# A batched matrix product: the deliberately uneven DMA load moved from the first store into the first x, and the last transposes moved forward

## Chip, cores, metric

One core of a Trainium2 chip. The metric is the device time of the program in microseconds (us), the lower the better. All runs told here are in the fast state. Ratios are the mean time of one kernel's fast runs over that of the other's of the same rounds, with a 95% interval, so they are not quite the ratio of the medians that are quoted beside them. The rounds ran on several chips; each ratio is to the kernel before on the same chip. A transfer is split over the 16 DMA engines; the part of one engine is called its share here, and a trace records when each share has landed.

## The reference

```python
def setup_inputs():
    batch, m, k, n = 32, 512, 1024, 768
    return {"x": randn(batch, m, k) as float32, "weight": randn(batch, k, n) as float32}

def reference(x, weight):
    return np.matmul(x, weight).astype(np.float32)
```

32 independent products of 512x1024 by 1024x768. The inputs are 168 MB and the output is 50 MB, so the time goes mainly into moving data.

## The kernel before

x and the weights are loaded on the GpSimd queue, which casts them to bf16, two batches of x and one batch of weights at a time. TensorE transposes x, multiplies, and the results go out as float32. Two details matter. The very first x is loaded as float32 by SyncE in one transfer. And a part of the first output is stored in 25 small transfers that use only a few DMA engines ("SKEWED").

```python
    w_pool = tile_pool(name="w", bufs=4);  x_pool = tile_pool(name="x", bufs=3)
    ...
    def transpose_first(mt):
        xT = xT_pool.tile([P, JT, P, 2], BF16, name="xT")
        for h in range(2):
            pt = tpsum.tile([P, JT, P], F32, name="pt")
            for i in range(JT):
                nc.tensor.transpose(pt[:, i, :], x_first[:, mt, JT * h + i::KT], ident)
            nc.vector.tensor_copy(...)          # cast to bf16
        return xT
    ...
    def store(b):
        cols = MT * N
        if b == SKEWED:
            cols -= 512
            for first in range(0, 120, 20):
                for at in range(first, first + 4):
                    rows = slice(at, first + 20, 4)             # 5 rows: 5 DMA engines
                    nc.sync.dma_start(out_view[b, rows, cols:], outs[b][rows, cols:])
            nc.sync.dma_start(out_view[b, 120:, cols:], outs[b][120:, cols:])
        nc.gpsimd.dma_start(out=out_view[b, :, :cols], in_=outs[b][:, :cols])

        x_first = x_pool.tile([P, MT, K], F32, name="x_sb")
        nc.sync.dma_start(x_first, x_view[0])
        load_w(0); load_pair(1); load_w(1); load_w(2); load_pair(3)
        for b in range(B):
            # GpSimd issues, in this order: the x pair ahead, load_w(b + 3), the store of b - 1
            ...
            if b == 0:
                xT = {mt: transpose_first(mt) for mt in range(MT)}
            elif b == B - 1:
                xT = {mt: transpose_last(mt) for mt in range(MT)}
            ...
```

A weight buffer is free for `load_w(b + 3)` only when TensorE is done with batch b - 1, and the x pair of batches 5 and 6 goes into the buffer of `x_first`. So the issue of loads follows TensorE.

Of the kernel before, what the change touches and what calls it, by code (L numbers as in the profile page):

```python
# [13 lines left out]
def kernel(  # L14
# [6 lines left out]
    nc = tc.nc  # L21
    B, M, K = x.shape
    _, _, N = weight.shape
    P = 128
    MT = M // P
    KT = K // P
# [3 lines left out]
    AHEAD = 3  # L30
    LATE = 4
    HELD = 3
    SKEWED = 0

    const = ctx.enter_context(tc.tile_pool(name="const", bufs=1))
    w_pool = ctx.enter_context(tc.tile_pool(name="w", bufs=4))
# [10 lines left out]
    x_view = x.rearrange("b (mi mo) k -> b mi mo k", mi=P)  # L47
    pair_view = x[1:B - 1].rearrange("(p r) (mi mo) k -> p (r mi) mo k", r=2, mo=2 * MT)
    out_view = out.rearrange("b (mi mo) n -> b mi (mo n)", mi=P)

    xs, ws, outs = {}, {}, {}

    def banks():
        return [mpsum.tile([P, 512], F32, name=f"pm{i}") for i in range(3)]

    def load_pair(b):

        xs[b] = x_pool.tile([P, 2 * MT, K], BF16, name="x_sb")
        nc.gpsimd.dma_start(out=xs[b], in_=pair_view[b // 2])  # L59

    def load_last():
        xs[B - 1] = x_pool.tile([P, MT, K], BF16, name="x_sb")
        nc.gpsimd.dma_start(out=xs[B - 1], in_=x_view[B - 1])  # L63

    def load_w(b):
        ws[b] = w_pool.tile([P, KT, N], BF16, name="w_sb")
        at = 0
        for n in CHUNKED.get(b, (KT,)):
            nc.gpsimd.dma_start(out=ws[b][:, at:at + n, :], in_=w_view[b, :, at:at + n, :])  # L69
            at += n  # L70


    def words(b, mo):
        pt = tpsum.tile([P, JT, P], F32, name="pt")
        pairs = xs[b].bitcast(F32)
        for j in range(JT):
            nc.tensor.transpose(pt[:, j, :], pairs[:, mo, j::JT], ident)  # L77
        return pt.bitcast(BF16)

    def transpose_pair(b, mt):  # L80

        both = xT_pool.tile([P, 2, JT, P // 2, 2, 2], BF16, name="xT")
        for half in range(2):
            nc.vector.tensor_copy(  # L84
                both[:, :, :, :, half, :].rearrange("p b j i r -> p j b i r"),
                words(b, mt + MT * half).rearrange("p j (b i r) -> p j b i r", b=2, r=2),
            )
        return [both[:, r].rearrange("p j i h r -> p j (i h) r") for r in range(2)]

    def transpose_last(mt):  # L90
        xT = xT_pool.tile([P, JT, P, 2], BF16, name="xT")
        nc.vector.tensor_copy(  # L92
            xT.rearrange("p j m r -> p (j m r)"), words(B - 1, mt).rearrange("p j m -> p (j m)")
# [10 lines that stand above are left out]
            nc.vector.tensor_copy(  # L104
                xT[:, 2 * h:2 * h + 2].rearrange("p j m r -> p j r m"),
                pt.rearrange("p (j r) m -> p j r m", r=2),
            )
        return xT
# [8 lines left out]
    def matmuls(pm, half, xT, b, kos, together):  # L117
        for ko in kos:
            for i, (bank, at, off, size) in enumerate(SPLITS[half]):
                shares = half == 1 and i == 0  # L120
                nc.tensor.matmul(  # L121
                    pm[bank][:, at:at + size],
                    xT[:, ko // 2, :, ko % 2],
                    ws[b][:, ko, off:off + size],
                    start=(ko == 0 and not (together and shares)),
                    stop=(ko == KT - 1),
                    skip_group_check=together,
                )

    def evacuate(b, pair, pm):  # L130
        o = outs[b][:, pair * N2:(pair + 1) * N2]
        nc.scalar.copy(o[:, 0:512], pm[0])  # L132
        nc.vector.tensor_copy(o[:, 512:1024], pm[1])  # L133
        nc.scalar.copy(o[:, 1024:N2], pm[2])  # L134

    def store(b):
        cols = MT * N
        if b == SKEWED:

            cols -= 512  # L140
            for first in range(0, 120, 20):
                for at in range(first, first + 4):
                    rows = slice(at, first + 20, 4)
                    nc.sync.dma_start(out_view[b, rows, cols:], outs[b][rows, cols:])
            nc.sync.dma_start(out_view[b, 120:, cols:], outs[b][120:, cols:])
        nc.gpsimd.dma_start(out=out_view[b, :, :cols], in_=outs[b][:, :cols])  # L146

    with tc.manual_schedule():
        x_first = x_pool.tile([P, MT, K], F32, name="x_sb")
        nc.sync.dma_start(x_first, x_view[0])  # L150
        load_w(0)
        ident = const.tile([P, P], F32)
        make_identity(nc, ident)
        load_pair(1)
        load_w(1)
        load_w(2)
        load_pair(3)

        ready = {}
        pending = []  # L160
        for b in range(B):
            if b % 2 and b + AHEAD + 1 < B:
                if b + AHEAD + 1 == B - 1:
                    load_last()
                else:
                    load_pair(b + AHEAD + 1)
            if b + AHEAD < B:
                load_w(b + AHEAD)
            if b <= B - LATE:
                if b > 0:  # L170
                    pending.append(b - 1)
                if b + AHEAD < B - HELD or b == B - LATE:
                    for at in pending:
                        store(at)
                    pending = []
            if b == B - 1:
                halves = [slice(pair * N2, (pair + 1) * N2) for pair in range(2)]
                nc.sync.dma_start(out_view[b - 1, :, halves[0]], outs[b - 1][:, halves[0]])
                for late in range(B - LATE, B - 2):
                    nc.sync.dma_start(out_view[late], outs[late])  # L180
                nc.sync.dma_start(out_view[b - 1, :, halves[1]], outs[b - 1][:, halves[1]])
            outs[b] = out_pool.tile([P, MT * N], F32, name="out_sb")
            if b == 0:
                xT = {mt: transpose_first(mt) for mt in range(MT)}
            elif b == B - 1:
                xT = {mt: transpose_last(mt) for mt in range(MT)}
            else:
                if b % 2:
                    for mt in range(MT):
                        ready[b, mt], ready[b + 1, mt] = transpose_pair(b, mt)  # L190
                xT = {mt: ready.pop((b, mt)) for mt in range(MT)}
            if b not in CHUNKED:
                for pair in range(2):
                    pm = banks()
                    for half in range(2):
                        matmuls(pm, half, xT[2 * pair + half], b, range(KT), False)
                    evacuate(b, pair, pm)
                continue
            pms = [banks() for _ in range(2)]
            at = 0  # L200
            for n in CHUNKED[b]:
                last = at + n == KT
                for mt in range(MT):
                    matmuls(pms[mt // 2], mt % 2, xT[mt], b, range(at, at + n), True)
                    if last and mt % 2 == 1:
                        pair = mt // 2
                        evacuate(b, pair, pms[pair])
                        if b == B - 1:
                            nc.sync.dma_start(out_view[b, :, halves[pair]], outs[b][:, halves[pair]])
                at += n  # L210
# [30 lines left out]
```

## Time and profile before

| | before |
|---|---|
| median of 6 runs (range) | 516.35 us (515.49 to 518.96) |
| HBM traffic | 218.1 MB, 423 GB/s over the span |
| TensorE busy | 85% |
| DMA engines | full from 2 us to about 510 us |
| slowest share of the last store lands | 515.0 us, the fastest 510.6 |

The page, the chain and the last stretches are shown in the prediction. Two more views matter afterwards: what TensorE waited for (total us, times, longest), and when GpSimd issued its transfers (start, duration, the wait ahead of it in brackets). In the views `pt` is the result of transposes, `pm` that of matmuls, `w_sb` weights and `x_sb` x.

```profile
PE pm L121 <- DMA w_sb<-in_weight_dram: 43.3, 12, 5.4
PE pt L103 <- DMA x_sb<-in_x_dram: 12.3, 1, 12.3
```

```profile
19.52 0.53 POOL L59 DMA_DIRECT2D x_sb<-in_x_dram  x1 [14.38 <-PE pt L103]
29.92 0.53 POOL L69 DMA_DIRECT2D w_sb<-in_weight_dram  x1 [9.87 <-PE pm L121]
...
45.98 0.53 POOL L69 DMA_DIRECT2D w_sb<-in_weight_dram  x1 [14.70 <-PE pm L121]
```

The x pair of batches 5 and 6 is issued at 19.5 us, the weights of batch 4 at 29.9 and those of batch 5 at 46.0. The queue ahead of them (six loads, all issued by 5.1 us, the last of which lands at 58 us) keeps the DMA engines supplied beyond these times.

### The profile page before, as it was taken

Reading aid. Unit: us, or ns where it says so; the run is one execution under the profiler, and the core shown is the slowest. Engines: PE = TensorE matmul, PEld = TensorE weight load, DVE = VectorE, ACT = ScalarE, POOL = GpSimd, SP = SyncE. Lnnn points to the kernel's source line nnn. Section 1 sums busy time; section 2 is a strip of 40 time slices with the busy share of each in tenths; the row PEclk is TensorE's granted clock in tenths of the full one; section 3 lists DMA queues with packets and bytes.
Section 4 is the critical chain, followed back from the end, with each engine's and each line's share of the span. In section 5 each row is a group of like instructions: output and inputs, shape, how many; then the busy total and the mean of one; then the engine's idle time right before and its main releaser. Section 6 shows DMA issues by size and latency. Waiting matters only on the chain.

```text
span 515.9 us, 5853 instructions
## 1 busy us (share of the span) xinstructions
PE 440.0 (85%) x2576; PEld 279.6 (54%) x2576; DVE 129.9 (25%) x196; ACT 76.2 (15%) x129; POOL 43.8 (8%) x87
## 2 busy tenths in 40 slices
PE   0999969979799697996979979898797988999992
PEld 0665635646366364663646636464464644656661
DVE  0541412314132041320413204141041410404131
ACT  0012111111111111111111111111111111111211
POOL 3001000010000100001000010000001100011000
PEclk9999998989899798997999979999798997999998
DMA  8999999999999999999999999999999999999996
GB/s 255 217 219 215 221 255 293 211 279 274 272 283 211 283 268 275 279 213 293 260 273 273 224 295 246 280 278 235 299 233 275 279 250 300 214 277 215 289 426 276
DMA packets 12952, 135.63 MB, mean 263 GB/s; under 512 B 1536, under 2 KB 1536, under 8 KB 3328
## 3 DMA queue, kind: packets, MB, share of 16 engines
q0 software_dynamic: 11664, 126.62, 96.2%
q1 hardware_dynamic: 1264, 8.65, 4.2%
q8 instruction: 20, 0.33, 0.2%
q14 instruction: 4, 0.03, 0.0%
HBM read 167.77 MB, written 50.33 MB: 423 GB/s over the span
## 4 chain that ended last, share of the span: by engine, by line
PE 64%; DMA 21%; DVE 7%; another core or an unknown queue 6%; issue 1%; ACT 0%
PE pm L121 56%; DMA w_sb<-in_weight_dram 19%; PE pt L77 6%; DVE xT L84 4%; DMA x_sb<-in_x_dram 2%; DVE out_sb L133 2%; PE pt L103 1%; DVE xT L104 0%; DVE xT L92 0%; ACT out_sb L134 0%
## 5 line engine op out<-in xcount | busy, mean ns | idle before, releaser
L121 PE MATMUL pm<-w_sb,xT 128*128 128x256 bf16 (+1 forms) x2048 | 358.9, 339 | 43.3 <-DMA w_sb<-in_weight_dram 43.3
L121 PEld LDWEIGHTS <-xT 128*128 128x128 bf16 x2048 | 206.8, 101 | 190.8 <-DMA w_sb<-in_weight_dram 47.9
L133 DVE COPY out_sb<-pm 128x512 f32<-128x512 f32 x64 | 44.3, 691 | 351.4 <-PE pm L121 338.4
L77 PE MATMUL pt<-ident,x_sb 128*128 128x128 f32 x496 | 79.8, 302 | 10.5 <-DVE xT L84 10.2
L132 ACT COPY out_sb<-pm 128x512 f32<-128x512 f32 x64 | 37.5, 585 | 305.9 <-PE pm L121 290.7
L77 PEld LDWEIGHTS pt<-ident,x_sb 128*128 128x128 f32 x496 | 69.3, 209 | 21.5 <-DVE xT L84 18.7
L84 DVE COPY xT<-pt 128x1024 bf16<-128x1024 bf16 x120 | 77.4, 687 | 11.0 <-PE pt L77 11.0
L134 ACT COPY out_sb<-pm 128x512 f32<-128x512 f32 x64 | 37.5, 585 | 124.0 <-PE pm L121 123.9
L69 POOL DMA_DIRECT2D w_sb<-in_weight_dram x37 | 19.7, 533 | 298.2 <-PE pm L121 261.4
L146 POOL DMA_DIRECT2D out_dram<-out_sb x28 | 15.0, 536 | 81.7 <-DMA w_sb<-in_weight_dram 41.9
L103 PE MATMUL pt<-ident,x_sb 128*128 128x128 f32 x32 | 6.7, 362 | 12.5 <-DMA x_sb<-in_x_dram 12.3
L103 PEld LDWEIGHTS pt<-ident,x_sb 128*128 128x128 f32 x32 | 5.1, 205 | 13.9 <-issue 12.2
L59 POOL DMA_DIRECT2D x_sb<-in_x_dram x15 | 8.0, 533 | 45.0 <-DMA out_dram<-out_sb 30.6
L104 DVE CAST xT<-pt 128x512 bf16<-128x512 f32 x8 | 5.8, 736 | 14.2 <-PE pt L103 13.8
L92 DVE COPY xT<-pt 128x1024 bf16<-128x1024 bf16 x4 | 2.6, 686 | 0.2 <-PE pt L77 0.2
L132 ACT ACT_TABLE_LOAD x1 | 1.3, 1283 | 0.7 <-PEq L225 0.7
L63 POOL DMA_DIRECT2D x_sb<-in_x_dram x1 | 0.5, 528 | 6.7 <-DMA w_sb<-in_weight_dram 6.7
masks.py:199 POOL TENSOR_SCALAR_AFFINE_SELECT ident<-ident 128x128 f32<-128x128 f32 x1 | 0.3, 287 | 0.1
masks.py:197 POOL MEMSET ident<- 128x128 f32 x1 | 0.2, 223 | 0.0
L225 POOL MEMSET const-float32-0.0<- 128x1 f32 x1 | 0.1, 98 | 0.2 <-issue 0.2
L225 POOL MEMSET const-bfloat16-1.0<- 128x1 bf16 x1 | 0.1, 101 | 0.0
L225 POOL MEMSET const-uint8-127<- 128x1 uint8 x1 | 0.1, 101 | 0.0
(1 smaller groups left out, 0.1 us busy)
## 6 DMA issues: line engine op xcount, KB each, us to landing
w_sb<-in_weight_dram POOLq DMA_DIRECT2D x28, 1536.0 KB, 47.3
out_dram<-out_sb POOLq DMA_DIRECT2D x27, 1536.0 KB, 46.6
x_sb<-in_x_dram POOLq DMA_DIRECT2D x15, 2048.0 KB, 52.4
w_sb<-in_weight_dram POOLq DMA_DIRECT2D x7, 768.0 KB, 38.4
out_dram<-out_sb SPq DMA_DIRECT2D x4, 768.0 KB
out_dram<-out_sb SPq DMA_DIRECT2D x2, 1536.0 KB
x_sb<-in_x_dram SPq DMA_DIRECT2D x1, 2048.0 KB
out_dram<-out_sb POOLq DMA_DIRECT2D x1, 1280.0 KB, 48.7
```

Of the source, the lines that this page charges most:

```text
L59: nc.gpsimd.dma_start(out=xs[b], in_=pair_view[b // 2])
L69: nc.gpsimd.dma_start(out=ws[b][:, at:at + n, :], in_=w_view[b, :, at:at + n, :])
L77: nc.tensor.transpose(pt[:, j, :], pairs[:, mo, j::JT], ident)
L84: nc.vector.tensor_copy(both[:, :, :, :, half, :].rearrange("p b j i r -> p j b i r"), words(b, mt + MT * half).rearrange("p j (b i r) -> ...
L92: nc.vector.tensor_copy(xT.rearrange("p j m r -> p (j m r)"), words(B - 1, mt).rearrange("p j m -> p (j m)"))
L103: nc.tensor.transpose(pt[:, i, :], x_first[:, mt, JT * h + i::KT], ident)
L104: nc.vector.tensor_copy(xT[:, 2 * h:2 * h + 2].rearrange("p j m r -> p j r m"), pt.rearrange("p (j r) m -> p j r m", r=2),)
L121: nc.tensor.matmul(pm[bank][:, at:at + size], xT[:, ko // 2, :, ko % 2], ws[b][:, ko, off:off + size], start=(ko == 0 and not (together an ...
L132: nc.scalar.copy(o[:, 0:512], pm[0])
L133: nc.vector.tensor_copy(o[:, 512:1024], pm[1])
L134: nc.scalar.copy(o[:, 1024:N2], pm[2])
L146: nc.gpsimd.dma_start(out=out_view[b, :, :cols], in_=outs[b][:, :cols])
```

## The change

Intent: have the uneven load in the first x instead of in the first store, start the first transposes after 1.5 MB instead of 2 MB, and hide the last transposes among the matmuls of batch 30.

```diff
-    def store(b):
-        ... 24 stores of 5 rows x 2 KB and one of 8 rows for b == SKEWED, the rest in one store
-
         x_first = x_pool.tile([P, MT, K], F32, name="x_sb")
-        nc.sync.dma_start(x_first, x_view[0])
+        nc.sync.dma_start(x_first[:, :MT - 1], x_view[0, :, :MT - 1])
+        few = [slice(at, first + 20, 4) for first in (0, 20, 40) for at in range(first, first + 4)]
+        for rows in (slice(64, P), slice(60, 64), *few):
+            nc.sync.dma_start(x_first[rows, MT - 1], x_view[0, rows, MT - 1])
...
-                        store(at)
+                        nc.gpsimd.dma_start(out=out_view[at], in_=outs[at])
...
-                xT = {mt: transpose_first(mt) for mt in range(MT)}
+                xT = {mt: transpose_first(mt) for mt in range(MT - 1)}
             elif b == B - 1:
-                xT = {mt: transpose_last(mt) for mt in range(MT)}
+                xT = last_xT
...
-                        matmuls(pm, half, xT[2 * pair + half], b, range(KT), False)
+                        mt = 2 * pair + half
+                        if mt not in xT:
+                            xT[mt] = transpose_first(mt)
+                        matmuls(pm, half, xT[mt], b, range(KT), False)
...
                 for mt in range(MT):
+                    if last and b == B - 2:
+                        last_xT[mt] = transpose_last(mt)
                     matmuls(pms[mt // 2], mt % 2, xT[mt], b, range(at, at + n), True)
```

More of the change, by code (lines that the diff above doesn't have):

```diff
@@ L32 @@
     HELD = 3
-    SKEWED = 0
     const = ctx.enter_context(tc.tile_pool(name="const", bufs=1))
@@ L134, in evacuate @@
         nc.scalar.copy(o[:, 1024:N2], pm[2])
-    def store(b):
-        cols = MT * N
-        if b == SKEWED:
-            cols -= 512
-            for first in range(0, 120, 20):
-                for at in range(first, first + 4):
-                    rows = slice(at, first + 20, 4)
-                    nc.sync.dma_start(out_view[b, rows, cols:], outs[b][rows, cols:])
-            nc.sync.dma_start(out_view[b, 120:, cols:], outs[b][120:, cols:])
-        nc.gpsimd.dma_start(out=out_view[b, :, :cols], in_=outs[b][:, :cols])
     with tc.manual_schedule():
         x_first = x_pool.tile([P, MT, K], F32, name="x_sb")
-        nc.sync.dma_start(x_first, x_view[0])
+        nc.sync.dma_start(x_first[:, :MT - 1], x_view[0, :, :MT - 1])
+        few = [slice(at, first + 20, 4) for first in (0, 20, 40) for at in range(first, first + 4)]
+        for rows in (slice(64, P), slice(60, 64), *few):
+            nc.sync.dma_start(x_first[rows, MT - 1], x_view[0, rows, MT - 1])
         load_w(0)
@@ L157 @@
         load_pair(3)
-        ready = {}
+        ready, last_xT = {}, {}
         pending = []
```

## The prediction

> **What bounds the kernel now.** I read the page first, then the chain that ended last in order of time, then the busy time by stretch at the end, then SyncE's own waits.
>
> ```profile
> span 515.9 us, 5853 instructions
> PE 440.0 (85%) x2576; PEld 279.6 (54%) x2576; DVE 129.9 (25%) x196; ACT 76.2 (15%) x129; POOL 43.8 (8%) x87
> ...
> DMA  8999999999999999999999999999999999999996
> ...
> HBM read 167.77 MB, written 50.33 MB: 423 GB/s over the span
> ```
>
> The DMA row is 9 from the second slice to the last but one: the 16 DMA engines are never short of work. TensorE is busy 85% of the time, so it has slack somewhere. The traffic is 218.1 MB whatever the order: 13.63 MB on each engine if it is spread evenly.
>
> The chain of waits looks different at its end:
>
> ```profile
> 423.55 3.59 another core or an unknown queue
> 427.14 0.05 issue
> 427.19 12.93 PE pm L121 x63
> ...
> 493.05 0.02 issue
> 493.07 0.70 DVE out_sb L133
> 493.78 0.69 DVE xT L92
> 494.46 0.04 issue
> 494.51 1.35 PE pt L77 x8
> 495.86 10.41 PE pm L121 x64
> 506.27 0.02 issue
> 506.29 0.58 ACT out_sb L134
> ```
>
> From 427 us TensorE waits for no data any more; the transposes of the last x (493.05 to 495.86) and the 64 matmuls of batch 31 stand on this chain, and it ends at 506.87. Taken alone it would promise that any microsecond saved there is saved at the end. But the span ends 9.0 us later, so the stretches after it have to be read:
>
> ```profile
> 500.00:507.00 7.00, 6.25 (x39) 3.54 (x37) 1.38 (x2) 2.30 (x4) 0.00 (x0) 1.00 0.96 408
> 507.00:510.00 3.00, 0.00 (x0) 0.00 (x0) 0.00 (x0) 0.00 (x0) 0.00 (x0) 1.00 1.01 420
> 510.00:513.00 3.00, 0.00 (x0) 0.00 (x0) 0.00 (x0) 0.00 (x0) 0.00 (x0) 0.65 0.51 211
> 513.00:515.00 2.00, 0.00 (x0) 0.00 (x0) 0.00 (x0) 0.00 (x0) 0.00 (x0) 0.50 0.08 34
> ```
>
> The last two columns are the DMA share and GB/s. The DMA engines are full until 510, then they run out one after another. The completion updates in the trace (one for each engine's share of a transfer) say who is last. The last store's 16 shares end at 510.6 to 513.1 for fourteen engines, and 514.5 and 515.0 for the other two. The latest shares of the last four stores end at 509.5, 511.3, 513.1 and 515.0: 1.83 us apart, for 48 KB each, 26.9 GB/s. So the slowest DMA engine has a backlog to the very end, although the last two stores were issued only at 505.6 and 506.9. The early engines instead had a gap (505.7, then 508.7, then 510.6). **The bound is the slowest DMA engine's total work**, and TensorE's end has about 4 us to spare: the slowest engine gets to the last two stores only at about 511.3.
>
> **What the Trainium skill says.** "DMA: Bandwidth & Descriptors", section "Measured", gives 425 GB/s for a 16 MB load; the 423 GB/s above agrees, so there is no rate left to win. Its section "Why a DMA increments its semaphore by 16 and not by 1" says that a transfer runs on the largest number of engines, up to 16, that divides the slowest dimension, and on SyncE's path on the lowest-numbered ones. So 5 rows go to engines 0 to 4, 64 rows to all 16, 4 rows to engines 0 to 3, 8 rows to 0 to 7. The trace agrees in count: 128 packets of 2 KB for 24 x 5 + 8 rows, and each small store shows five completions. After them, in the store at 77 to 79.5 us, five shares are late (79.1 to 79.5, the others 76.9 to 78.2), where earlier transfers had all 16 within 1 us. Its section "Queues, rings and completion order" says that an engine takes turns between queues packet by packet. The trace agrees:
>
> ```profile
> 30.27 37.17 SPq L144 DMA_DIRECT2D out_dram<-out_sb  x24
> 68.27 0.33 SPq L145 DMA_DIRECT2D out_dram<-out_sb  x1
> ```
>
> The small stores landed from 36.0 to 78 us, some 2.0 us apart, far more than 2 KB need: each has two packets (data, completion), and each waits for a GpSimd-queue packet of 0.93 us (a weight row) or 1.23 us (an x row).
>
> **The change, part by part.**
>
> *1. The uneven loading is moved, not altered.* Before: 24 stores of 5 rows x 2 KB and one of 8 rows. Engines 0 to 4 carry 25 x 2 = 50 KB instead of 16 KB (+34 KB), engines 5 to 7 2 KB (-14), engines 8 to 15 none (-16). After: the first x's last row tile is 4 KB a row; an even split would be 32 KB. 64 rows give every engine 16 KB; 4 rows give 4 KB to engines 0 to 3; 12 loads of 5 rows give 48 KB to engines 0 to 4. So engines 0 to 3 have 68 KB (+36), engine 4 64 KB (+32), engines 5 to 15 16 KB (-16). Against before: +2 KB, -2 KB, -2 KB, 0. At 26.9 GB/s 2 KB are 0.08 us. Whichever engine is the slowest, its sum changes by less than 0.1 us. A few packets and completions more or fewer (22 ns each): under 0.3 us.
>
> *2. The start of batch 0.* The first load shrinks from 2.0 to 1.5 MB. Before, it landed at 12.1, the transposes ran 12.27 to 19.2, and the matmuls began when they ended, w having landed at 15.8. After, three tiles are in by about 9.5, transposed by about 15 (24 of 32 transposes, 5.2 of 6.95 us), and the matmuls begin at about 15.5 to 16, some 3 us earlier. Then the fourth tile is missing. Queue turns put its arrival late: the 64 rows take five turns of about 1 us after 5.6 us, the 4 rows two, the 12 small loads 12 x 2 turns at about 2.0 us a load = 24 us: about 34 to 40 us. TensorE wants it at about 24. So I expect TensorE to stand still for 10 to 15 us there, batch 0 to end at 38 to 44 instead of 29.64, and the next x pair (issued at 19.5, when x_first is free) and w of batch 4 (29.9) to be issued as much later.
> Does the DMA queue run dry? No: the fourth weight load lands at 58 before, so the next transfer in the queue, the x pair, is wanted only at about 50. w of batch 5, issued at 46, landed at 87 behind transfers that end at 79.5; issued at 60 it is still in time. TensorE, 12 us late, catches up in the waits for w which it has (43.3 us in 12 waits). By about 150 us it is on the old timetable. Cost at the end: 0.
>
> *3. The last x.* x of batch 31 lands at 474.6; its transposes move from after 493.05 to between the matmuls of batch 30 from 488 on. No new wait. 16 transposes cost 16 x 0.121 = 1.9 us of TensorE wherever they stand; the waits for VectorE between them go (2.60 us from the first transpose to the first matmul, so 0.3 to 0.7 us). TensorE ends at about 506.3 instead of 506.87. Batch 30's two halves are evacuated 1 and 2 us later, and SyncE's stores (491.3 on) start about 1 us later, while the slow engine has GpSimd-queue stores in hand until 504.0. Effect at the end: 0, as the slow engine has 4 us of backlog.
>
> *4. The first store* goes from 1280 to 1536 KB in one transfer, the 256 KB taken from the small stores: counted in 1.
>
> Sum: 0 +- 0.4 us in the slowest engine's work. Prediction 516.8, which is the old median of 517.0 with a token 0.2 off.
>
> **Rivals.** (a) *TensorE's chain sets the end.* For it: the chain of waits from 427 us on. Then the 0.3 to 0.7 us of part 3 come off, and the time is 516.4. Against: the 1.83 us steps of the last stores. (b) *The late fourth tile starves the DMA queue* or the delay lives on to 427 us: the weight loads wait for TensorE's buffers (261.4 us of GpSimd's waits). Each microsecond of dry queue is one at the end; 1 to 5 us, 518 to 522. Against: some 46 us from issue to landing, four weight buffers. (c) *Where the uneven load stands matters*: it sits on five engines from 10 us on instead of from 36 on and takes loads instead of stores, and the slowest engine at the end may be one of the five or not. If the drift between engines (0.7 us of spread at 15 us, 5.6 us at 474) depends on who lags, the end moves by up to 2 us either way, 514.8 to 518.8. Nothing in the profile tells, as it doesn't name engines.
>
> **Range and chances.** The three runs before lie between 515.5 and 519.0, a scatter larger than any term above; it and rival (c) make the range, 514.8 to 518.8. 2% would be 10.3 us: as the bytes on the slowest engine are the same, nothing here can give that, and only a queue dry for 10 us could cost it. Faster by over 2%: 0.01; within 2%: 0.98; slower: 0.01.
>
> **What would show the steps right or wrong.** Right: the DMA row stays at 9; the last store's latest shares end 1.83 us apart; TensorE's first matmul on w at about 16, a gap of 10 us or more before the last 8 transposes of x_first, and later waits for w summing to some 10 us less; the last transposes without VectorE waits; the last matmul about 0.5 us earlier with the span unchanged. Wrong: a DMA slice below 9 between 40 and 120 us (rival b), last stores that start in gaps on all engines (rival a), or a spread of the last store's shares well off 4.4 us (rival c).

## The result and the profile after

| | before | after |
|---|---|---|
| median (range), 6 runs each | 516.35 us (515.49 to 518.96) | 520.01 us (518.30 to 521.52) |
| ratio | | 1.0066 (1.0037 to 1.0096) |

The change costs 3.4 us, and the median lies above the predicted range. The page of the changed kernel:

```profile
span 518.3 us, 5792 instructions
...
DMA  8999999999999999999999999999999999999996
...
HBM read 167.77 MB, written 50.33 MB: 421 GB/s over the span
```

The DMA row looks exactly as before. One slice is 13 us long and 9 means 90% or more, so a loss of one microsecond is invisible there. The waits of TensorE and its order in time show at once where to look:

```profile
PE pt L102 <- DMA x_sb<-in_x_dram: 39.9, 1, 39.9
PE pm L120 <- DMA w_sb<-in_weight_dram: 26.6, 7, 5.1
```

```profile
39.86 5.43 PE L102 MATMUL pt<-ident,x_sb 128*128 128x128 f32 x24 [39.86 <-DMA x_sb<-in_x_dram]
45.13 7.96 PE L120 MATMUL pm<-w_sb,xT 128*128 128x512 bf16 x47
52.93 1.05 PE L102 MATMUL pt<-ident,x_sb 128*128 128x128 f32 x8
54.36 2.77 PE L120 MATMUL pm<-w_sb,xT 128*128 128x256 bf16 x16 [0.38 <-DVE xT L103]
```

The first transpose starts at 39.86 us, not at 12.27 as before and not at 9.5 as predicted. The 1.5 MB load had landed at about 10 us. But the 24 transposes of the first three row tiles waited for the last of the 12 small loads too, which landed at 39.6. There is then no gap before the last 8 transposes (52.93): everything waited at the start. Batch 0 ends at 57.1, 27.5 us later than before, and GpSimd's issues follow:

```profile
54.28 0.53 POOL L58 DMA_DIRECT2D x_sb<-in_x_dram  x1 [49.14 <-PE pt L102]
57.43 0.53 POOL L68 DMA_DIRECT2D w_sb<-in_weight_dram  x1 [2.62 <-PE pm L120]
...
73.50 0.53 POOL L68 DMA_DIRECT2D w_sb<-in_weight_dram  x1 [14.71 <-PE pm L120]
```

The fourth weight load, the last transfer in the queue, was finished by the first DMA engine at 56.0 us. The x pair behind it was issued only at 54.28. Busy time in the stretches 54 to 60 and 70 to 76 us, before and then after (the last two columns are DMA share and GB/s):

```profile
54.00:60.00 6.00, 5.52 (x37) 4.38 (x35) 3.61 (x6) 0.58 (x1) 1.06 (x2) 1.00 1.07 228
70.00:76.00 6.00, 2.15 (x13) 1.08 (x11) 0.69 (x1) 0.65 (x2) 0.53 (x1) 1.00 0.98 269
```

```profile
54.00:60.00 6.00, 5.15 (x33) 3.80 (x33) 3.71 (x7) 0.59 (x1) 1.59 (x3) 1.00 0.98 197
70.00:76.00 6.00, 5.95 (x38) 3.66 (x38) 0.69 (x1) 1.45 (x3) 1.60 (x3) 1.00 0.99 174
```

The loss has two parts. At 54 to 60 us engines really have nothing to do for a moment: between 56.0 and 56.5, on average 10.4 packets are under way instead of 16.5, and the first packets of the x pair then take up to 2.05 us instead of 1.23. At 70 to 76 us the share is full, but packets of the weight load take up to 2.6 us instead of 0.93. A "busy" DMA engine may thus be slow, and GB/s has to be read beside the share. (The GB/s before at 70 to 76 is higher also because stores, which count fully, begin there earlier; for weights the row counts the bf16 bytes written, some 212 GB/s at full rate.)

Where the loss arises shows from the landing times. The median of the 16 shares of each transfer was 0.5 us earlier than before at the fourth weight load (56.4 against 56.9; the kernel before had by then also moved eleven small stores), 0.6 later at the x pair (67.2 against 66.6), 1.9 later at the weights of batch 4 (76.2 against 74.3), 2.7 later at the first store (80.1 against 77.4), and still about 2.5 later at 215 us. So some 2.5 us are lost between 56 and 80 us and are not won back; the two profiled executions differ by 2.4 us in all (518.3 against 515.9). A pair of runs told below, `changed_again` against `contig12`, is cleaner, as both have the same transfers on the same chip: 0.0 us at the fourth weight load, then 1.2, 2.8 and 2.9 later, and 2.8 at 155 us. The slowest share, which sets the end, wanders more: in the first pair it was 1.4 us late at 80 us, 0.0 at 300 and 2.2 at the end; in the second 2.5, 3.8 and (at 500 us) 3.9. So not all of the end's delay is traced to 56 to 80 us.

At the end, the slowest share of the last four stores lands at 511.7, 513.5, 515.3 and 517.2: 1.83 us apart, as before.

### The profile page after: what moved, and what is told of

Its sections match the earlier page's. It is cut to its first block, busy times and chain, and to the rows that moved or that the text cites. A ratio compares the mean times of both kernels' runs of the same rounds, so it can differ in the third digit from the quotient of the medians.

```text
span 518.3 us, 5792 instructions
## 1 busy us (share of the span) xinstructions
PE 427.7 (83%) x2528; PEld 277.2 (53%) x2576; DVE 129.8 (25%) x196; ACT 76.3 (15%) x129; POOL 43.8 (8%) x87
## 4 chain that ended last, share of the span: by engine, by line
PE 61%; DMA 25%; DVE 6%; another core or an unknown queue 3%; issue 1%; SPq 1%; ACT 0%
PE pm L120 54%; DMA w_sb<-in_weight_dram 19%; DMA x_sb<-in_x_dram 7%; PE pt L76 6%; DVE xT L83 4%; DVE out_sb L132 2%; PE pt L102 1%; SPq L141 1%; DVE xT L103 0%; ACT out_sb L133 0%; SPq L138 0%
## 5 line engine op out<-in xcount | busy, mean ns | idle before, releaser
L120 PE MATMUL pm<-w_sb,xT 128*128 128x256 bf16 (+1 forms) x2000 | 347.9, 333 | 29.5 <-DMA w_sb<-in_weight_dram 26.6
L120 PEld LDWEIGHTS <-xT 128*128 128x128 bf16 x2048 | 204.3, 100 | 167.5 <-DMA w_sb<-in_weight_dram 29.3
L76 PEld LDWEIGHTS pt<-ident,x_sb 128*128 128x128 f32 x496 | 69.5, 209 | 21.1 <-DVE xT L83 18.7
L102 PE MATMUL pt<-ident,x_sb 128*128 128x128 f32 x32 | 6.5, 369 | 39.9 <-DMA x_sb<-in_x_dram 39.9
```

Source lines behind the costliest of these rows:

```text
L76: nc.tensor.transpose(pt[:, j, :], pairs[:, mo, j::JT], ident)
L120: nc.tensor.matmul(pm[bank][:, at:at + size], xT[:, ko // 2, :, ko % 2], ws[b][:, ko, off:off + size], start=(ko == 0 and not (together an ...
```

## The experiments

Theory A: the first transposes wait for the small loads; so TensorE frees its buffers late, the next loads are issued late, and the DMA queue runs short between 55 and 76 us. Theory B: moving the last transposes delays the last stores. Theory C: the uneven load is worse in the first x than in the first store. All ran with 5 rounds beside the kernel before.

### The two parts of the change apart

`last_only` is the kernel before with only the last part of the diff (`last_xT`). `first_only` is the changed kernel without it.

> The kernel before with the second part of the change alone: the last x is transposed among the last matmuls of batch 30. Theory A (dry queue: the late first x delays the loads after the fourth weight load, and the DMA engines run short of work from 55 to 76 us): this part costs nothing, ratio to before 1.000 +- 0.002, and the x of batch 0 lands as before. Theory B (the later stores of batch 30 at the end cost the 3 us): ratio 1.005 or more. Last matmul about 0.6 us earlier than in the kernel before under both.

> The changed kernel with the last x transposed where it was before, so the first part of the change alone. Theory A (dry queue at 55 to 76 us): the whole loss is here, ratio 1.006 to 1.007. Theory B (later stores of batch 30): ratio 1.000 to 1.002.

Measured: `last_only` 515.75 us, ratio 1.0004 (0.9984 to 1.0024); `first_only` 519.19 us, ratio 1.0063 (1.0046 to 1.0081). The loss comes with the first part; theory B, which asked for 1.005 or more in `last_only`, falls. `first_only` shows both marks of the changed kernel, an x pair issued at 54.53 and weight packets of up to 2.5 us from 70 us on. What the last part does on TensorE is seen in the chain of `last_only`:

```profile
485.18 0.47 PE pt L77 x4
...
486.95 0.48 PE pt L77 x4
...
488.73 0.47 PE pt L77 x4
...
490.50 0.48 PE pt L77 x4
```

The transposes take 1.90 us of the chain, where before 2.81 us passed from 493.05 to 495.86. 0.9 us are saved on TensorE, and the time doesn't move.

### The late tile in a buffer of its own

```diff
-        x_first = x_pool.tile([P, MT, K], F32, name="x_sb")
+        x_first = x_pool.tile([P, MT - 1, K], F32, name="x_sb")
+        x_late = out_pool.tile([P, MT * N], F32, name="out_sb")[:, :K]
...      (the small loads go to x_late, transpose_first(3) reads it)
```

> The changed kernel with the last row tile of the first x in a buffer of its own, so that the first transposes wait for the 1.5 MB load alone; the same small loads, the same uneven loading. Theory A (dry queue because the first transposes wait for all 15 loads): first transpose at about 9 to 10 us instead of 39.9, batch 0 ends at about 44 instead of 57.4, the next x pair is issued at about 15, no stretch with idle DMA engines at 55 to 76 us, and the ratio comes back to 1.000 +- 0.002. Theory C (the uneven load stands worse in the first x than in the first store): the ratio stays at 1.005 or more.

Measured: 516.91 us, ratio 1.0022 (0.9997 to 1.0047), correct. Same bytes, same small loads on the same engines:

```profile
10.45 5.68 PE L103 MATMUL pt<-ident,x_sb 128*128 128x128 f32 x24 [10.45 <-DMA x_sb<-in_x_dram]
...
39.95 1.94 PE L103 MATMUL pt<-ident,out_sb 128*128 128x128 f32 x8 [16.02 <-DMA out_sb<-in_x_dram]
```

This is the timetable that the prediction had for the changed kernel: first transpose at 10, a stop of 16 us before the fourth tile, batch 0 done at 45. The x pair is issued at 16.4, the weights of batch 4 at 45.6, and neither idle engines nor long packets appear at 54 to 76 us. By the mean, two thirds of the loss of `first_only` are gone. The interval just reaches 1.000, so whether some 0.2% remain is open, and it just touches that of `first_only`; the separation that leaves no doubt comes with `contig12`.

### Why the first transposes waited: one slice

Transposes of row tiles 0 to 2 read nothing that the small loads write. The built program has the wait all the same: its first transpose waits for all eight of SyncE's completion counters, which count the 15 loads of the first x. (Built again, `contig12`, `few_big` and `own_tile` wait there for one counter, that of the 1.5 MB load.) `contig12` alters only which rows a small load takes:

```diff
-        few = [slice(at, first + 20, 4) for first in (0, 20, 40) for at in range(first, first + 4)]
+        few = [slice(at, at + 5) for at in range(0, 60, 5)]
```

> The changed kernel with one slice altered: the 12 small loads take 5 neighbouring rows each (0 to 4, 5 to 9, ...) instead of every fourth row of 20. Bytes, number of loads, engines and packet turns are the same. The built program's first transpose then waits for the 1.5 MB load alone; with rows of step 4 it waits for all 15 loads. Theory A: first transpose at about 10.3 instead of 39.9, the fourth tile still at about 40 (12 small loads), batch 0 done at about 45, no dry queue, ratio 1.000 to 1.002. If the waiting for all 15 loads were not the cause: ratio 1.006 as the changed kernel's.

Measured: 516.76 us over 11 runs, ratio 1.0016 (0.9999 to 1.0032). On the same chip and in the same rounds the changed kernel ran again:

> The changed kernel again, beside the others on the same chip: ratio 1.006 to 1.007, DMA engines short of work from 55 to 57 us and weight packets longer than 0.93 us at 70 to 76 us, as in its first profile.

Measured: 520.42 us, ratio 1.0097 (1.0083 to 1.0110), above the expected ratio; on this chip the loss was 4 us by the medians and 5 by the ratio. The marks are the same (x pair issued at 54.36, weight packets stretched at 70 to 76 us). `contig12`, first on TensorE, then the two stretches:

```profile
10.30 5.35 PE L102 MATMUL pt<-ident,x_sb 128*128 128x128 f32 x24 [10.30 <-DMA x_sb<-in_x_dram]
...
39.89 1.94 PE L102 MATMUL pt<-ident,x_sb 128*128 128x128 f32 x8 [16.18 <-DMA x_sb<-in_x_dram]
```

```profile
54.00:60.00 6.00, 6.00 (x39) 3.66 (x38) 0.69 (x1) 1.76 (x3) 0.00 (x0) 1.00 1.07 227
70.00:76.00 6.00, 5.51 (x36) 4.25 (x35) 3.27 (x6) 0.92 (x2) 1.07 (x2) 1.00 1.00 303
```

With neighbouring rows, the framework that places the waits does not order the small loads before the reads of the first three row tiles; with every fourth row it does, although they don't overlap. So the cause of the 3 to 5 us is the step of 4 in a row slice. TensorE still stands for 16 us, and that costs nothing measurable. Theory C falls with this run too, as an account of the 3 us: the uneven load is in the first x, on the same engines, without the loss.

### Fewer, larger small loads

```diff
-        few = [slice(at, first + 20, 4) for first in (0, 20, 40) for at in range(first, first + 4)]
+        few = [slice(0, 25), slice(25, 50), slice(50, 55), slice(55, 60)]
```

> The changed kernel with the same bytes on the same five engines, but rows 0 to 59 of the last row tile in 4 loads (25, 25, 5 and 5 rows) instead of 12 of 5: 16 packet turns on each of these engines instead of 24. Theory A: the last of the first x lands at about 30 instead of 39.7, everything of batch 0 comes some 9 us earlier than in the changed kernel, the x pair is issued at about 45, the weights of batch 4 at about 48, so no dry queue, ratio 1.000 to 1.002. Theory C (place of the uneven load): the ratio stays at 1.005 or more.

Measured: 515.65 us, ratio 1.0017 (0.9994 to 1.0041). The time came out as expected, but partly for another reason: since these rows are neighbours as well, the first transpose did not wait (10.31 us), which I had overlooked when I wrote the expectation and which led to `contig12`. The part on the queue's turns held: the fourth tile was there at 33.3 us instead of 39.9 (expected about 30), the x pair was issued at 35.6 and the weights of batch 4 at 39.0.

### The dose: TensorE held in the kernel before

Here nothing of the change is in the program. The kernel before gets one matmul that reads a later load and so holds TensorE until this has landed:

```diff
             if b == 0:
+                held = tpsum.tile([P, JT, P], F32, name="pt")
+                nc.tensor.matmul(held[:, 0, :], ws[2][:, 0, 0:P], ws[2][:, 0, 0:P], start=True, stop=True)
```

`stall40` reads `ws[2]`, `stall50` reads `xs[3]`, `stall58` reads `ws[3]`.

> The kernel before, all its transfers as they are, but one added matmul that reads the weights of batch 2 holds TensorE until they have landed, at about 40 us, before the first transpose. Theory A: the weights of batch 4 are issued at about 57.5 and those of batch 5 at about 73.5, as in the changed kernel, but the next x pair at about 47 instead of 54.3; so the DMA engines run short again, a part of the 3.4 us or all of it comes: ratio 1.002 to 1.007. Theory C (place of the uneven load): ratio 1.000.

> As stall40 and stall58, TensorE held until the x of batches 3 and 4 has landed, at about 50 us. Theory A: x pair issued at about 57.7 (1.5 us after the fast engines have run out, at 56), weights of batch 4 at 68, of batch 5 at 84 when the first store has ended at 80 to 81: dry for 3 us and again for 4 to 5 us, so ratio between those of stall40 (1.003) and stall58 (1.036): 1.010 to 1.018.

> As stall40, but TensorE is held until the weights of batch 3 have landed, at about 58 us. Theory A (dry queue): the next x pair is issued at about 66, the weights of batch 4 at 76 and of batch 5 at 92, so the DMA engines stand idle from about 57 to 67 and again for some 4 us before 93: 9 to 15 us more than before, ratio 1.018 to 1.030. If TensorE's lateness itself counted, or nothing of it, the time would rise by 28 us less the waits, or not at all.

Beside the measured loss (ratio less 1, times 516 us) the table has, from the DMA packets of each trace between 54 and 102 us: idle time (engines without a packet under way, as us of all 16) and long packets (what packets over their usual length took beyond it, as us of all 16).

| kernel | x pair issued | w of batch 4 | w of batch 5 | ratio (95%) | loss, us | idle, us | long packets, us |
|---|---|---|---|---|---|---|---|
| before | 19.5 | 29.9 | 46.0 | 1 | 0 | 0.0 | 0.2 |
| contig12 | 42.1 | 46.3 | 62.3 | 1.0016 (0.9999 to 1.0032) | 0.8 | 0.0 | 0.0 |
| stall40 | 47.9 | 58.3 | 74.4 | 1.0028 (1.0008 to 1.0048) | 1.4 | 0.1 | 1.5 |
| changed | 54.3 | 57.4 | 73.5 | 1.0066 (1.0037 to 1.0096) | 3.4 | 0.4 | 1.7 |
| changed_again | 54.4 | 57.5 | 73.6 | 1.0097 (1.0083 to 1.0110) | 5.0 | 0.4 | 1.7 |
| stall50 | 57.0 | 67.4 | 83.5 | 1.0216 (1.0202 to 1.0230) | 11.1 | 5.5 | 4.4 |
| stall58 | 64.7 | 75.1 | 91.2 | 1.0362 (1.0344 to 1.0380) | 18.7 | 13.3 | 4.0 |

In `stall58` the queue is plainly dry:

```profile
54.00:60.00 6.00, 2.86 (x13) 2.36 (x13) 1.47 (x2) 0.00 (x0) 0.00 (x0) 1.00 0.32 68
```

(`stall40` ran on another chip than `contig12`, `changed_again`, `stall50` and `stall58`.) The later the loads are issued, the more is lost, and the knee lies where theory A puts it: a TensorE that is 16 us late (`contig12`) costs nothing that these runs can tell from zero, one that is 28 us late (`stall40` and the changed kernel) 1 to 5 us, one that is 45 us late (`stall58`) 19 us. Beyond the knee it is one for one: `stall58` issues the x pair 7.7 us later than `stall50` and loses 7.6 us more. `stall40` and the changed kernel issue the weights at almost the same times and differ mainly in the x pair (47.9 against 54.3), the transfer for which the queue ran dry at 56. Both larger stalls cost more than I had expected (2.2% and 3.6% against at most 1.8% and 3.0%). The expectations counted idle engines only; the long packets add some 4 us to each. In both, idle time and long packets explain all but some 1.3 us of the loss. In the changed kernel they give 2.1 of 3.4, in its repeat 2.1 of 5.0; the rest is not accounted for.

What makes packets long is not settled. A dry queue beforehand is not needed: in `stall40` they begin at 71 us, though until 83.9 us never fewer than 15 packets were under way. So what the runs show is that a late issue costs the time; the dry moment of theory A is only 0.4 us of it in the changed kernel, and the larger part, the long packets, has no known mechanism. They are there in all six profiles in which the weights of batch 4 were issued after 57 us (1.5 to 4.4 us in all), 0.1 us or less in `contig12`, `few_big`, `own_tile`, `own_even` and `double_skew`, and there in a small measure (0.2 to 0.5 us at 70 to 74) in three kernels with an early issue, before, `last_only` and `no_skew`.

### What the uneven load is worth

`no_skew` is the kernel before with `SKEWED = -1`. `own_even` is `own_tile` with the fourth row tile in one load of 128 rows. `double_skew` is `few_big` with the small stores of the kernel before as well.

> The kernel before without the small stores: the first output is stored in one even transfer. If the slowest DMA engine is not one of the five, it has 16 KB or 0.6 us more to do: ratio 1.001. If it is one of the five, it has 34 KB or 1.3 us less: ratio 0.998. This tells what the uneven load is worth at most.

> own_tile with the fourth row tile loaded in one even transfer of 128 rows: no uneven load, no small loads. First transpose at about 10, batch 0 done at about 28. Theory A: no dry queue, so the ratio equals that of no_skew within 0.002, although TensorE starts 2 us earlier.

> An attempt to beat both kernels: the uneven load of the changed kernel (as 4 loads of neighbouring rows, with no long wait) and that of the kernel before (25 small stores) together, so twice the shift from eleven engines to five. no_skew against before gave 1.0024 for one shift. If the slowest engine is still one of the eleven: ratio 0.998. If the five become the slowest: 1.002 or more.

Measured: `no_skew` 516.47 us, ratio 1.0024 (1.0005 to 1.0043); `own_even` 516.19 us, 1.0012 (0.9998 to 1.0025); `double_skew` 515.79 us, 0.9994 (0.9982 to 1.0006). The uneven load of the kernel before is worth about 0.2%, 1.2 us, with an interval that holds the 0.6 us worked out from its bytes. A start of the transposes at 10.1 us instead of 12.3 buys nothing that these runs show (`own_even` against `no_skew`: the intervals overlap). Twice the uneven load is no faster on average than once; what it did change is the scatter: 13 runs between 515.72 and 515.85, where the kernel before had 23 between 515.14 and 518.16 in these rounds. Its last store's shares end with the slowest 0.6 us behind the next, so which engine is last may have become fixed; that is an argument only. No version beat the kernel before beyond the noise.

With the uneven load in the first x, `contig12`, `own_tile` and `few_big` have the ratios 1.0016, 1.0022 and 1.0017: by these means it is worth no more than no uneven load at all (1.0024 and 1.0012). But the fastest runs of these three took 515.0 to 515.4 us, like those of the kernel before (515.0 to 515.1), against 516.0 and 516.3 in `own_even` and `no_skew`. Whether the uneven load does as much in the first x as in the first store stays open at this size.

## Why the prediction was wrong, point by point

- **The bound** was right: the DMA engines' work, up to the slowest engine's last share in steps of 1.83 us, before and after. `last_only` speaks against TensorE's chain: 0.9 us shorter, same time, though its interval, from 0.9984, only just excludes a gain of 0.9 us (0.9983). Rival (a) fell.
- **Part 1** (uneven load moved, not altered) was right within the noise: with the same uneven load in the first x and no long wait, `contig12` is within noise of before. Rival (c) is not the loss; an effect of 0.2% is open, as told above.
- **Part 2 failed**, in two places. The step "three tiles are in by about 9.5, transposed by about 15" assumed that a transpose waits for the loads of the tile it reads. It waited for all 15 loads, until 39.86. I had not read TensorE's waits in the built program, and it stood there: the first transpose waits for eight counters. The arrival of the last small load, "about 34 to 40 us", was right (39.6; 2.0 us for each small load). What was off is the order of things: the 1.5 MB tiles' transposes and 48 of the 64 matmuls of batch 0 were to run before that moment and ran after it. So batch 0 ended at 57.1 instead of "38 to 44". A smaller slip stands beside it: the x pair was to be issued "as much later" as TensorE stands still, 10 to 15 us after 19.5, but its buffer is free only when the fourth tile is transposed, so after 34 to 40 by the prediction's own count. `contig12` measured 42.1: even without the long wait the margin before "about 50" was only 8 us.
- From there **"Does the DMA queue run dry? No"** fell with it. The argument was sound (the x pair is "wanted only at about 50"), and the runs place the limit between an x pair issued at 47.9 (`stall40`: no engine idle at 56) and one issued at 54.3 (the changed kernel: idle engines). Rival (b) was the right one in its path, from the late x to the late issue, and "1 to 5 us, 518 to 522" was the right size; but only 0.4 us of it is a dry queue. I had dismissed it on a timetable that depended on the unchecked wait.
- "By about 150 us it is on the old timetable" was wrong too: TensorE's first wait for weights ended at 237 us, against 76 us before. No loss is seen from it: the median landings stay 2.1 to 2.8 us late from 80 to 280 us.
- **Part 3** was right in effect and slightly undersized: 0.9 us saved on TensorE against 0.3 to 0.7.
- The check that I named, "a DMA slice below 9 between 40 and 120 us", could not have shown it: a slice of 13 us hides a gap of half a microsecond. For the same reason "never short of work" was more than the DMA row can say.

## What to carry to other kernels

Where the transfers are the bound and always busy, as here, a late compute engine costs little until it frees its buffers later than the queue's backlog lasts; work out that time first. Here each microsecond well beyond it was lost (7.7 us later, 7.6 us lost). When one buffer is filled by several loads, read in the built program what the first reader really waits for: here rows with a step made the framework order every load ahead of every read, and neighbouring rows did not. And read DMA share and GB/s together in windows of a few microseconds, since the page's slices hide a short drought.

## What the Trainium skill lacked or had wrong

- "DMA: Bandwidth & Descriptors", section "Queues, rings and completion order", says that an engine takes turns between queues, but not what a small transfer then costs beside a full queue. Here the small loads of five 4 KB rows landed 2.0 us apart on average (12 loads, 1.1 to 2.6 us apart, the last at 39.6 us), and the 2 KB stores before 1.8.
- The same page has nothing on packets that take longer when loads are issued late, with all engines busy: weight packets took up to 2.6 us instead of 0.93 at 70 to 76 us, some 1.5 us of all 16 engines beside the 0.4 us of idle time. The mechanism is open.
- "Perfetto Trace Analysis", section "Identifying the Most-Contended Engine", warns that the occupancy of 16 DMA engines misleads, but gives no example; the runs do: at 70 to 74 us, where almost only weights are loaded, the changed kernel's share was 1.14 with 175 GB/s, where packets of the usual length give 212 (16 engines, 12,288 bytes in 0.926 us).
- No page that I read says what a wait placed for overlapping parts of one buffer covers; here a step of 4 in the rows moved the first transpose from 10.3 to 39.9 us.
